# A graph attention layer on one core: TensorE fill-in work, run counts moved into the merges, shorter keys, and bins laid out by tile

## The chip, the cores and the metric

The kernel runs on one core of a Trainium2 chip. A core has five engines, each with its own instruction stream: TensorE (PE, matrix multiply; PEld is its weight load), VectorE (DVE), ScalarE (ACT), GpSimd (POOL) and SyncE (SP), which only issues transfers here. They share a fast memory of 128 partitions, TensorE writes into a separate accumulator memory (PSUM), and sixteen DMA engines move data to and from the chip's main memory (DRAM). The metric is the device time of one execution in microseconds (us); smaller is better.

## The reference

A graph attention layer with 4096 nodes, 50000 edges, 4 heads and 64 features in and out:

```python
x_proj[h] = x @ weight[h]
score[h, e] = sum(x_proj[h, src[e]] * att_src[h]) + sum(x_proj[h, dst[e]] * att_dst[h])
score = where(score > 0, score, 0.2 * score)
output[h, dst[e]] += exp(score[h, e]) * x_proj[h, src[e]]          # over all edges
output[h, dst]    /= sum(exp(score[h, e]) for e into dst) + 1e-8   # per node with edges
```

The result is the heads side by side, 4096 x 256, in float32.

## The kernel before

The kernel sorts the edges so that the work becomes matrix multiplies with one-hot matrices. The order of the work is the order in which the code issues it (a manual schedule); each engine runs its own stream in that order and waits on semaphores.

**Keys and first sort.** The edges' source and destination ids arrive in two halves, on SP's and ACT's queues. DVE makes one float key of each edge (L695 to L698, four instructions for each half): the high bits of the source (one of 16 source groups of 256 nodes), then the destination, then the low 8 bits of the source. Meanwhile ACT counts how many sources lie below each group's bound (`below`, L269). Then `Sorter.rows` sorts each partition's 391 keys with compare steps, and `Sorter.runs` merges eight partitions into one sorted run. A `half` step (L201) is two instructions, a minimum and a maximum over 128x256 elements, and the next step needs both. The loop over m (L245) has two stages, m = 1 and m = 2; each ends with nine `half` steps, or fewer when the last bits need no order (`fine`). A list `between` holds small closures; one is called after each of the last steps of stage m = 2.

**Where each group starts.** `counts` multiplies the counted signs with a selection matrix on TensorE (L280). `bounds` turns the result into start and end positions `ws1` and `we1`, by 14 small DVE instructions (L289 to L295). The sorted keys are stored to DRAM (L261, SP), `fetch` casts the positions to integers (L352), and GpSimd gathers each group's stretch of each run by two indirect transfers (L354).

**Tables.** Beside the first sort, `tables` makes on TensorE and ACT the node tables `xa` and `adb` that the matrix multiplies read later (L404 to L425).

**Second sort.** `group` merges the fetched stretches in the same way, so that each source group (16 of them, one to each tile) has its edges by destination. Here the small count steps already stand between the last merge steps, as do `relative` and `split`, which make the bins of block 0. TensorE runs 80 small matmuls into a tile `turn` (L372) before the counts of this sort and 5 wide ones into a tile `warm` (L377) behind them; their results are not used. `warm` and the counts share one PSUM buffer.

**Blocks.** The destinations are cut into 33 blocks of 125. An edge's bin is a pair (row: destination within the block; column: source within the group), and a block has 16 tiles of 128 edges each. For a block b:

- `load` (L472, SP) brings the block's bins to all partitions, 8 KB to each: 2 halves (row, column) x 16 tiles x 128. Blocks 0 and 1 get theirs through TensorE instead: `spread` (L483), with copies from PSUM by ACT or DVE (L485).
- `onehot` (DVE) compares the bins with the partition number: half 0 is one instruction over rows and columns (L498, 4096 elements), half 1 compares the columns again with the number plus 128 (L501, 2048 elements).
- `gather` (TensorE, L519, L521, L525, in three chunks of 6, 6 and 4 tiles) picks source features and scores; ACT takes `ex` (L527) and `xs` (L529) out of PSUM.
- `weights` (L539) and `values` (L547) on DVE make weighted features; `sums` (L563, L570) adds them up by destination into the PSUM tile `acc`; `take` (ACT, L624, L626), `project` (TensorE, L631), `invert` and `give` (DVE, L636, L644) finish a block, and SP stores it.

**The handover to the blocks.** The bins of blocks 2 and up pass through DRAM. GpSimd gathers five windows of the second sort's result (`Windows`, L354), window i for blocks 8i to 8i+7. `unpack(i)` splits a window into rows and columns (L442, L443 on DVE, L446, L447 on DVE for window 0 and on GpSimd for the others) and SP writes both to `gat_bins` (L449, two transfers to a window). The code from L729 on orders it: block 0 by `spread`, the windows, `longest` (L334 to L338), `unpack(0)`, loads of blocks 2 to 4, block 1 by `spread`, then `unpack(1)` to `unpack(4)`, `sums(0, 1)`, `onehot(2)`, and the loop `run(1)` over the other blocks. DVE's stream therefore has the four unpacks ahead of `onehot(2)`, and TensorE's first work for block 2 waits for that. The name `gather(b, c)` below means chunk c of block b.

Of the kernel before, what the change touches and what calls it, by code (L numbers as in the profile page):

```python
# [11 lines left out]
P = 128  # L12
# [9 lines left out]
L = 512  # L22
# [16 lines left out]
def kernel(ctx: ExitStack, tc: tile.TileContext, x: bass.AP, edge_index: bass.AP,  # L39
# [21 lines left out]
    skey2 = nc.dram_tensor("gat_sorted2", (1, P * L + W2), I32).ap()  # L61
    bin_dram = nc.dram_tensor("gat_bins", (8 * NI, 2, NR, W2), BF16).ap()

# [98 lines left out]
    adb = cst.tile([P, ND, AB], BF16)  # L162
    Wbd = cst.tile([P, 2, P], F32)
    ws1 = cst.tile([P, 2], F32)
    we1 = cst.tile([P, 2], F32)
# [6 lines left out]
    class Sorter:  # L172
# [58 lines left out]

        def runs(self, to=None, fine=0, between=()):

            s, d = self.step()
            V.stream_shuffle(out=self.z[:], in_=s[:], mask=[p ^ 1 for p in range(32)])
            V.tensor_scalar(out=self.y[:], in0=s[:], scalar1=sig[:, 0:1], scalar2=None, op0=OP.mult)
            V.scalar_tensor_tensor(out=d[:], in0=av(self.z[:], L - 1, [-1, L]), scalar=sig[:, 0:1], in1=self.y[:],
                                   op0=OP.mult, op1=OP.min)  # L240
            s, d = self.step()
            V.tensor_scalar(out=d[:], in0=s[:], scalar1=sj[0][:, 0:1], scalar2=None, op0=OP.mult)
            for j in range(8, -1, -1):
                self.half(j)
            for m in range(1, 3):  # L245
                self.turn()
                self.opposed(m)
                for j in range(m - 1, -1, -1):
                    self.half(j)
                self.turn()  # L250
                last = fine if m == 2 else 0
                todo = list(between) if m == 2 else []
                for j in range(8, last - 1, -1):
                    self.half(j, to=to if m == 2 and j == last else None)
                    if todo:
                        todo.pop(0)(self.a[self.cur])
                assert not todo
            return to or self.a[self.cur]
# [24 lines left out]

    def bounds(pool, cps, nt, n, off, mask, nk, ws, we):

        ni = ws.shape[1] // len(cps)
        for i, ps in enumerate(cps):
            cnt = pool.tile([P, nt + 1], F32, name=f"cnt{i}")
            V.tensor_scalar(out=cnt[:], in0=ps[:], scalar1=-0.5, scalar2=RUN * n / 2, op0=OP.mult, op1=OP.add)  # L289
            for o, t in ((0, ws), (1, we)):  # L290
                pick = pool.tile([P, ni, nk], F32, name=f"pick{i}{o}")
                V.tensor_tensor(out=pick[:], in0=av(cnt[:], o, [nk, ni], [1, nk]),
                                in1=av(mask[:], 0, [0, ni], [1, nk]), op=OP.mult)
                V.tensor_reduce(out=t[:, i * ni:(i + 1) * ni], in_=pick[:], axis=AX, op=OP.add)
                V.tensor_tensor(out=t[:, i * ni:(i + 1) * ni], in0=t[:, i * ni:(i + 1) * ni],  # L295
                                in1=av(off[:], i, [0, ni]), op=OP.add)

# [58 lines left out]

    PAGE = 80

    def group(pool, pp, start, between=()):

# [6 lines left out]
        so.rows(9)  # L367
        if between:

            turn = pp.tile([P, L], F32, name="turn")  # L370
            for i in range(PAGE):
                T.matmul(out=turn[:, 0:32], lhsT=identb[:], rhs=identb[:, 0:32], start=True, stop=True)  # L372
        st = Stretches(pool, counts(pool, pp, sgn, 8 * NI, [sel2[:]])[0])
        if between:
            warm = pp.tile([P, L], F32, name="warm")
            for i in range(5):
                T.matmul(out=warm[:], lhsT=identb[:], rhs=adb[:, 0:4, 0:P], start=True, stop=True)  # L377
        ki = pool.tile([P, L], I32, name="ki")
# [52 lines left out]
    class Windows:  # L431
# [7 lines left out]

        def unpack(self, i, *engs):  # L440
            t, tb = self.t[:, i], self.tb[:, i]
# [5 lines left out]
            e.tensor_scalar(out=tb[:, 0, :], in0=t[:, 0, :], scalar1=boff[:, i:i + 1], scalar2=None, op0=OP.add)  # L447
            for k, eng in enumerate(engs):
                eng.dma_start(out=dataclasses.replace(bin_dram[8 * i, k], ap=[[2 * NR * W2, 8], [W2, NR], [1, W2]]),  # L449
                              in_=self.tb[:, i, k, :])  # L450

# [5 lines left out]
    class Blocks:  # L457
# [11 lines left out]
        def load(self, b):  # L469
            if b < ND:  # L470
                t = self.bcp.tile([P, 2, NT * W2], BF16, name="bc")
                nc.sync.dma_start(out=t[:], in_=dataclasses.replace(bin_dram[b], ap=[[0, P], [NT * W2, 2],  # L472
                                                                                    [1, NT * W2]]))
                self.bc[b] = t

        def spread(self, b, c, tb, row, copy):

            if c == 0:
                self.bc[b] = self.bcp.tile([P, 2, NT * W2], BF16, name="bc")
            t0, n = CH[c]  # L480
            ps = self.psx.tile([P, CH[0][1], PW], F32, name="ps")
            for i in range(n):
                T.matmul(out=ps[:, i, :], lhsT=av(identb[:], row(t0 + i), [0, P]), rhs=tb, start=(i % 2 == 0),  # L483
                         stop=True, skip_group_check=True)
            copy(out=av(self.bc[b][:], t0 * W2, [W2, n], [NT * W2, 2], [1, W2]),  # L485
                 in_=av(ps[:], 0, [PW, n], [W2, 2], [1, W2]))

        def onehot(self, b, t0=0, nt=NT, halves=(0, 1)):
            if b >= ND:
                return  # L490
            if t0 == 0 and halves[0] == 0:

                self.oh[b] = self.bp.tile([P, 3, NT * W2], BF16, name="oh")
            oh, bc = self.oh[b], self.bc[b]
            e = slice(t0 * W2, (t0 + nt) * W2)
            for i in halves:
                if i == 0:
                    V.tensor_scalar(out=oh[:, 0:2, e], in0=bc[:, :, e], scalar1=pF[:, 0:1], scalar2=None,  # L498
                                    op0=OP.is_equal)
                else:  # L500
                    V.tensor_scalar(out=oh[:, 2, e], in0=bc[:, 1, e], scalar1=pF[:, 1:2], scalar2=None,  # L501
                                    op0=OP.is_equal)

        def gather(self, b, c):
# [9 lines left out]
            t0, n = CH[c]  # L514
            ps = self.psx.tile([P, CH[0][1], PW], F32, name="ps")
            for i in range(n):
                t = t0 + i
                e = slice(t * W2, (t + 1) * W2)
                T.matmul(out=ps[:, i, P:P + XC], lhsT=oh[:, 1, e], rhs=xa[:, 2 * t, :], start=(i % 2 == 0), stop=False,  # L519
                         skip_group_check=True)  # L520
                T.matmul(out=ps[:, i, 0:S0], lhsT=oh[:, 0, e], rhs=adb[:, b, :], start=False, stop=False,  # L521
                         skip_group_check=True)
            for i in range(n):
                t = t0 + i
                T.matmul(out=ps[:, i, P:P + XC], lhsT=oh[:, 2, t * W2:(t + 1) * W2], rhs=xa[:, 2 * t + 1, :],  # L525
                         start=False, stop=True, skip_group_check=True)
            S.activation(out=av(ex[:], 2 * t0, [2, n], [2 * NT, 2 * H], [1, 2]),  # L527
# [152 lines left out]
    with tc.tile_pool(name="sort1", bufs=1) as so1, tc.tile_pool(name="pre", bufs=1) as pr, \  # L680
            tc.tile_pool(name="pps", bufs=2, space=PSUM) as pps, \
            tc.tile_pool(name="pp1", bufs=1, space=PSUM) as pp1:
        sli = so1.tile([P, EL], I32)
        tF = so1.tile([P, EL], F32)
        uF = so1.tile([P, EL], F32)
# [5 lines left out]
        for e, n in ((0, EH), (EH, EL - EH)):  # L691
            src = av(eS[:], 2 * e, [2, n])
            dst = av(eD[:], 2 * e, [2, n])
            c = slice(e, e + n)
            V.tensor_scalar(out=sli[:, c], in0=src, scalar1=SG - 1, scalar2=None, op0=OP.bitwise_and)  # L695
            V.tensor_scalar(out=tF[:, c], in0=sli[:, c], scalar1=1.0 - N, scalar2=None, op0=OP.mult)
            V.scalar_tensor_tensor(out=uF[:, c], in0=dst, scalar=float(SG), in1=tF[:, c], op0=OP.mult, op1=OP.add)
            V.scalar_tensor_tensor(out=key[:, c], in0=src, scalar=float(N), in1=uF[:, c], op0=OP.mult, op1=OP.add)  # L698
        tables(pr, pps, pp1)
        so.rows(1, EL)  # L700
        cps = counts(so1, pp1, sgn, NR, [sel1[:, 0, :], sel1[:, 1, :]])
        store(skey1, so.runs())
        bounds(so1, cps, NR, EL, off1, m16, NR, ws1, we1)
    with ExitStack() as st:
# [3 lines left out]
        class Lent:  # L708


            def tile(self, shape, dt, name):
                return blocks.sink.psf.tile(shape, dt, name=name, tag="pf")


# [13 lines left out]

        stretches = group(so2, Lent(), ws1[:], (relative, split))  # L729
        win = Windows(cst, stretches.to[0][:])  # L730
# [6 lines left out]
        V.scalar_tensor_tensor(out=over[:], in0=most[:, 1:2], scalar=float(W2), in1=over[:], op0=OP.is_gt, op1=OP.max)  # L737
        win.unpack(0, nc.sync, nc.sync)
        for b in range(2, 5):
# [14 lines left out]
        for i in range(1, NI):  # L754
            win.unpack(i, nc.sync, nc.sync)
        blocks.sums(0, 1)
        blocks.onehot(2)
        blocks.weights(1)
# [5 lines left out]
    with tc.If(again > 0):  # L764
        n1 = room(0, EL)
        with tc.tile_pool(name="all", bufs=1) as al:
            total = al.tile([P, ND, AW], F32)
            V.memset(total[:], 0.0)
            with tc.For_i(0, n1, W1):
# [5 lines left out]
                with tc.For_i(0, m2, W2):  # L775
                    with ExitStack() as st:
                        win = Windows(st.enter_context(tc.tile_pool(name="win", bufs=1)), advance(al, ws2, we2, W2, 2)[:])
                        for i in range(NI):
                            win.unpack(i, nc.sync, nc.scalar)
                        blocks = Blocks(st, Total(total))  # L780
# [42 lines left out]
```

## Time and profile before

| | us |
|---|---|
| median of 4 runs | 292.77 |
| lowest and highest run | 291.27 and 293.16 |
| the profiled execution | 292.4 |
| its span (first to last instruction) | 290.4 |
| DVE busy in it | 261.4 (90%) |
| PE busy | 203.0 (70%) |
| ACT busy | 190.9 (66%) |
| POOL busy | 33.7 (12%) |

Times in the profile's views count from the start of the span; what lies around the span in the profiled execution is 2.0 us. A row of a timeline gives start, busy time, engine, source line, operation, tiles, and in brackets the idle time of the engine just before and what ended it. The chain of waits (part 4 of the page) has no entries in this profile, so the path has to be read from the rows of the engines.

### The profile page before, as it was taken

Reading aid. Unit: us, or ns where it says so; the run is one execution under the profiler, and the core shown is the slowest. Engines: PE = TensorE matmul, PEld = TensorE weight load, DVE = VectorE, ACT = ScalarE, POOL = GpSimd, SP = SyncE. Lnnn points to the kernel's source line nnn. Section 1 sums busy time; section 2 is a strip of 40 time slices with the busy share of each in tenths; the row PEclk is TensorE's granted clock in tenths of the full one; section 3 lists DMA queues with packets and bytes.
Section 4 is the critical chain, followed back from the end, with each engine's and each line's share of the span. In section 5 each row is a group of like instructions: output and inputs, shape, how many; then the busy total and the mean of one; then the engine's idle time right before and its main releaser. Section 6 shows DMA issues by size and latency. Waiting matters only on the chain.

```text
span 290.4 us, 8664 instructions
## 1 busy us (share of the span) xinstructions
PE 203.0 (70%) x3593; PEld 195.2 (67%) x3593; DVE 261.4 (90%) x528; ACT 190.9 (66%) x392; POOL 33.7 (12%) x81
## 2 busy tenths in 40 slices
PE   0001899990000017559999999999999999999980
PEld 0000599990000004459999999999999999999980
DVE  5999999996499999968999999999999999999960
ACT  2960720031499955755888888888888888888850
POOL 7882000000200000851000000000000000000000
PEclk9999975555555557997999999999999999999997
DMA  3026000001100000197776676768675767665011
GB/s 110 0 50 115 0 2 0 0 3 37 36 0 0 0 0 37 45 308 272 272 269 236 255 259 234 273 225 286 214 297 205 302 224 270 251 244 182 23 39 40
DMA packets 13328, 40.77 MB, mean 140 GB/s; under 512 B 3120, under 2 KB 8912, under 8 KB 9312
## 3 DMA queue, kind: packets, MB, share of 16 engines
q1 hardware_dynamic: 10768, 37.91, 36.0%
q10 hardware_dynamic: 1808, 1.56, 2.3%
q0 software_dynamic: 704, 0.66, 1.4%
q8 instruction: 30, 0.49, 0.7%
q14 instruction: 18, 0.15, 0.2%
HBM read 35.08 MB, written 5.05 MB: 138 GB/s over the span
## 4 chain that ended last, share of the span: by engine, by line


## 5 line engine op out<-in xcount | busy, mean ns | idle before, releaser
L529 ACT CAST xs<-ps 128x1200 bf16<-128x1200 f32 (+1 forms) x99 | 104.1, 1052 | 0.0
L547 DVE TENSOR_TENSOR val<-xs,wv 128x4096 bf16<-128x4096 bf16 (+1 forms) x34 | 75.4, 2221 | 0.4 <-ACT xs L529 0.2
L519 PE MATMUL ps<-xa,oh 128*128 128x72 bf16 x528 | 59.4, 197 | 5.0 <-DVE oh L498 3.4
L521 PE MATMUL ps<-adb,oh 128*128 128x136 bf16 x528 | 62.2, 225 | 0.0
L570 PE MATMUL acc<-xs,val 128*128 128x125 bf16 x1024 | 61.9, 218 | 0.0
L570 PEld LDWEIGHTS <-val 128*128 128x128 bf16 x1056 | 59.0, 98 | 0.1
L521 PEld LDWEIGHTS <-oh 128*128 128x128 bf16 x528 | 49.5, 99 | 1.7 <-issue 1.6
L519 PEld LDWEIGHTS <-oh 128*128 128x128 bf16 x528 | 47.3, 99 | 3.9 <-DVE oh L498 3.9
L498 DVE TENSOR_SCALAR oh<-bc,pF 128x4096 bf16<-128x4096 bf16 (+2 forms) x37 | 42.5, 1150 | 0.7 <-ACT bc L485 0.7
L527 ACT ACTIVATE ex<-ps 128x96 bf16<-128x96 f32 (+1 forms) x99 | 25.0, 252 | 24.8 <-PE ps L525 24.7
L201 DVE TENSOR_TENSOR sA<-sB 128x256 f32<-128x256 f32 (+2 forms) x104 | 37.2, 400 | 1.7
L201 DVE TENSOR_TENSOR sB<-sA 128x256 f32<-128x256 f32 (+2 forms) x98 | 35.1, 400 | 1.6
L525 PE MATMUL ps<-xa,oh 128*128 128x72 bf16 x528 | 33.7, 199 | 0.1
L280 PE MATMUL cnt_ps<-sgn,sel 128*128 128x17 f32 (+1 forms) x6 | 1.7, 390 | 40.1 <-ACT sgn L272 40.1
L280 PEld LDWEIGHTS cnt_ps<-sgn,sel 128*128 128x128 f32 x6 | 1.4, 319 | 40.1 <-issue 40.1
L525 PEld LDWEIGHTS <-oh 128*128 128x128 bf16 x528 | 26.6, 99 | 0.2 <-DVE oh L501 0.2
L501 DVE TENSOR_SCALAR oh<-bc,pF 128x2048 bf16<-128x2048 bf16 (+2 forms) x37 | 25.7, 694 | 0.0
L421 PEld LDWEIGHTS at_ps<-uv,xT 64*128 64x128 f32 x130 | 25.2, 302 | 0.2 <-issue 0.2
L421 PE MATMUL at_ps<-uv,xT 64*128 64x4 f32 x130 | 25.3, 331 | 0.0
L269 ACT ACTIVATE junk<-kr,nb 128x512 f32<-128x512 f32 x33 | 23.8, 722 | 1.1
L631 PE MATMUL pf<-Wbd,aT 128*128 128x128 f32 x132 | 22.8, 296 | 0.8 <-ACT aT L624 0.8
L404 PE MATMUL ps<-ident,wS 64*128 64x64 f32 x2 | 0.7, 350 | 27.9 <-DMA wS<-in_weight_dram 27.9
(144 smaller groups left out, 247.1 us busy)
## 6 DMA issues: line engine op xcount, KB each, us to landing
bc<-gat_bins SPq DMA_DIRECT2D x31, 1024.0 KB
out_dram<-res SPq DMA_DIRECT2D x32, 125.0 KB
eS<-in_edge_index_dram SPq DMA_DIRECT2D x2, 195.0 KB
eD<-in_edge_index_dram ACTq DMA_DIRECT2D x2, 195.0 KB
gat_bins<-tb SPq DMA_DIRECT2D x10, 32.0 KB
gat_sorted<-sA SPq DMA_DIRECT2D x1, 256.0 KB
gat_sorted<-ki SPq DMA_DIRECT2D x1, 256.0 KB
win<-gat_sorted,to POOLq DMA_INDIRECT x5, 2.6
```

The lines of the kernel that those rows point to most:

```text
L201: V.tensor_tensor(out=av(d[:], o, [2 * h, n], [1, h]), in0=av(s[:], 0, [2 * h, n], [1, h]), in1=av(s[:], h, [2 * h, n], [1, h]), op=op)
L269: S.activation(out=junk[:], in_=v, func=ACTF.Sign, bias=nbnd[:, b:b + 1], scale=1.0, accum_out=sgn[:, b:b + 1])
L421: T.matmul(out=ps[:, b, :], lhsT=xT[:, b * step:b * step + P], rhs=uv[:, k, :], start=(b == 0), stop=True, skip_group_check=True)
L498: V.tensor_scalar(out=oh[:, 0:2, e], in0=bc[:, :, e], scalar1=pF[:, 0:1], scalar2=None, op0=OP.is_equal)
L501: V.tensor_scalar(out=oh[:, 2, e], in0=bc[:, 1, e], scalar1=pF[:, 1:2], scalar2=None, op0=OP.is_equal)
L519: T.matmul(out=ps[:, i, P:P + XC], lhsT=oh[:, 1, e], rhs=xa[:, 2 * t, :], start=(i % 2 == 0), stop=False, skip_group_check=True)
L521: T.matmul(out=ps[:, i, 0:S0], lhsT=oh[:, 0, e], rhs=adb[:, b, :], start=False, stop=False, skip_group_check=True)
L525: T.matmul(out=ps[:, i, P:P + XC], lhsT=oh[:, 2, t * W2:(t + 1) * W2], rhs=xa[:, 2 * t + 1, :], start=False, stop=True, skip_group_check=True)
L527: S.activation(out=av(ex[:], 2 * t0, [2, n], [2 * NT, 2 * H], [1, 2]), in_=av(ps[:], P, [PW, n], [1, 2 * H], [0, 2]), func=ACTF.Exp)
L529: S.copy(out=xs[:, t0:t0 + n, 0:P + XC], in_=ps[:, 0:n, 0:P + XC])
L547: V.tensor_tensor(out=av(val[:], h * Dout, [Dout, n], [C, NT], [1, Din]), in0=av(xs[:], S0, [0, n], [XW, NT], [1, Din]), in1=av(wv[:], h * ...
L570: T.matmul(out=self.to[k], lhsT=val[:, t, k * P:(k + 1) * P], rhs=xs[:, t, 0:BD], start=apart and t == 0, stop=(t == NT - 1), skip_group_c ...
```

## The change

It has five parts.

1. **Keys.** The source's high bits are masked out in place of its low bits, so the key needs three instructions for each half, and the tile `tF` is gone.
2. **Counts.** `counts` of the first sort is issued to TensorE ahead of `tables`. `bounds` returns a list of 15 closures (the cast to integers `wi1` is the last) in place of running them; nine of them stand between the nine steps of stage m = 1 (`ahead`) and six between those of m = 2.
3. **TensorE.** The 80 small `turn` matmuls go. A function `busy(n)` issues n matmuls of 512 columns into a tile that shares its buffer with `acc`: 9 behind the counts of the second sort (5 before), 11 ahead of `unpack(0)`, where TensorE's stream goes on to `spread(1, ...)`, and 3 between `sums(0, 1)` and `gather(2, 0)`.
4. **Bins.** `gat_bins` and the tiles `bc` and `oh` are laid out by tile: 128 rows, then 128 columns, tile after tile. `unpack` writes a window by one transfer, 512 bytes to each partition, and `load` reads 8 KB in one piece where it read two of 4 KB. The copies behind `spread` become contiguous.
5. **One-hot.** Half 0 runs over one contiguous stretch. Half 1 reads the columns of `bc` in runs of 128 with gaps of 128 between them, and writes contiguously.

The diff, cut to its core:

```diff
-    bin_dram = nc.dram_tensor("gat_bins", (8 * NI, 2, NR, W2), BF16).ap()
+    bin_dram = nc.dram_tensor("gat_bins", (8 * NI, NR, 2, W2), BF16).ap()
...
-        def runs(self, to=None, fine=0, between=()):
+        def runs(self, to=None, fine=0, between=(), ahead=()):
...
-                todo = list(between) if m == 2 else []
+                todo = list(between if m == 2 else ahead)
...
-    def bounds(pool, cps, nt, n, off, mask, nk, ws, we):
+    def bounds(pool, cps, nt, n, off, mask, nk, ws, we, wi):
+        steps = []
...
-            V.tensor_scalar(out=cnt[:], in0=ps[:], scalar1=-0.5, scalar2=RUN * n / 2, op0=OP.mult, op1=OP.add)
+            steps.append(lambda cnt=cnt, ps=ps: V.tensor_scalar(
+                out=cnt[:], in0=ps[:], scalar1=-0.5, scalar2=RUN * n / 2, op0=OP.mult, op1=OP.add))
...
+        steps.append(lambda: V.tensor_copy(out=wi[:], in_=ws[:]))
+        return [lambda keys, f=f: f() for f in steps]
...
-            turn = pp.tile([P, L], F32, name="turn")
-            for i in range(PAGE):
-                T.matmul(out=turn[:, 0:32], lhsT=identb[:], rhs=identb[:, 0:32], start=True, stop=True)
         st = Stretches(pool, counts(pool, pp, sgn, 8 * NI, [sel2[:]])[0])
         if between:
-            warm = pp.tile([P, L], F32, name="warm")
-            for i in range(5):
-                T.matmul(out=warm[:], lhsT=identb[:], rhs=adb[:, 0:4, 0:P], start=True, stop=True)
+            busy(9)
...
-            for k, eng in enumerate(engs):
-                eng.dma_start(out=dataclasses.replace(bin_dram[8 * i, k], ap=[[2 * NR * W2, 8], [W2, NR], [1, W2]]),
-                              in_=self.tb[:, i, k, :])
+            nc.sync.dma_start(out=bin_dram[8 * i:8 * i + 8].rearrange("b g k e -> (b g) k e"), in_=tb)
...
-                t = self.bcp.tile([P, 2, NT * W2], BF16, name="bc")
-                nc.sync.dma_start(out=t[:], in_=dataclasses.replace(bin_dram[b], ap=[[0, P], [NT * W2, 2],
-                                                                                    [1, NT * W2]]))
+                t = self.bcp.tile([P, 2 * NT * W2], BF16, name="bc")
+                nc.sync.dma_start(out=t[:], in_=dataclasses.replace(bin_dram[b], ap=[[0, P], [1, 2 * NT * W2]]))
...
-            copy(out=av(self.bc[b][:], t0 * W2, [W2, n], [NT * W2, 2], [1, W2]),
-                 in_=av(ps[:], 0, [PW, n], [W2, 2], [1, W2]))
+            copy(out=self.bc[b][:, t0 * PW:(t0 + n) * PW], in_=av(ps[:], 0, [1, n * PW]))
...
-                    V.tensor_scalar(out=oh[:, 0:2, e], in0=bc[:, :, e], scalar1=pF[:, 0:1], scalar2=None,
-                                    op0=OP.is_equal)
+                    e = slice(2 * t0 * W2, 2 * (t0 + nt) * W2)
+                    V.tensor_scalar(out=oh[:, e], in0=bc[:, e], scalar1=pF[:, 0:1], scalar2=None, op0=OP.is_equal)
                 else:
-                    V.tensor_scalar(out=oh[:, 2, e], in0=bc[:, 1, e], scalar1=pF[:, 1:2], scalar2=None,
-                                    op0=OP.is_equal)
+                    V.tensor_scalar(out=av(oh[:], (2 * NT + t0) * W2, [W2, nt], [1, W2]),
+                                    in0=av(bc[:], (2 * t0 + 1) * W2, [2 * W2, nt], [1, W2]),
+                                    scalar1=pF[:, 1:2], scalar2=None, op0=OP.is_equal)
...
-            V.tensor_scalar(out=sli[:, c], in0=src, scalar1=SG - 1, scalar2=None, op0=OP.bitwise_and)
-            V.tensor_scalar(out=tF[:, c], in0=sli[:, c], scalar1=1.0 - N, scalar2=None, op0=OP.mult)
-            V.scalar_tensor_tensor(out=uF[:, c], in0=dst, scalar=float(SG), in1=tF[:, c], op0=OP.mult, op1=OP.add)
-            V.scalar_tensor_tensor(out=key[:, c], in0=src, scalar=float(N), in1=uF[:, c], op0=OP.mult, op1=OP.add)
+            V.tensor_scalar(out=sli[:, c], in0=src, scalar1=2 * N - SG, scalar2=None, op0=OP.bitwise_and)
+            V.scalar_tensor_tensor(out=uF[:, c], in0=sli[:, c], scalar=float(N - 1), in1=src, op0=OP.mult, op1=OP.add)
+            V.scalar_tensor_tensor(out=key[:, c], in0=dst, scalar=float(SG), in1=uF[:, c], op0=OP.mult, op1=OP.add)
+        cps = counts(so1, pp1, sgn, NR, [sel1[:, 0, :], sel1[:, 1, :]])
         tables(pr, pps, pp1)
         so.rows(1, EL)
-        cps = counts(so1, pp1, sgn, NR, [sel1[:, 0, :], sel1[:, 1, :]])
-        store(skey1, so.runs())
-        bounds(so1, cps, NR, EL, off1, m16, NR, ws1, we1)
+        steps = bounds(so1, cps, NR, EL, off1, m16, NR, ws1, we1, wi1)
+        store(skey1, so.runs(ahead=steps[:9], between=steps[9:]))
...
+        def busy(n):
+            t = blocks.psa.tile([P, L], F32, name="warm", tag="acc")
+            for i in range(n):
+                T.matmul(out=t[:], lhsT=identb[:], rhs=adb[:, 0:4, 0:P], start=True, stop=True)
...
+        busy(11)
+        win.unpack(0)
...
             win.unpack(i)
         blocks.sums(0, 1)
+        busy(3)
         blocks.onehot(2)
```

## The prediction

> **What bounds the kernel now.** I read the busy tenths first, then DVE's groups by shape, then the timeline around the two sorts and the handover.
>
> ```profile
> span 290.4 us, 8664 instructions
> ...
> PE   0001899990000017559999999999999999999980
> ...
> DVE  5999999996499999968999999999999999999960
> ...
> PEclk9999975555555557997999999999999999999997
> ```
>
> A slice is 7.26 us. DVE is full except at the start, around 70 us (slices 10 and 11), around 120 to 135 (17 to 19) and at the end. The granted clock is half from slice 6 to slice 15 and dips again in slice 18. In the loop from about 142 us DVE has no idle time; a block takes 4.71 us and PE, full too, 4.70. So I follow DVE to 142 us; what it gains until then, the end gains, unless an instruction in the loop becomes dearer.
>
> **The keys.** The second half of the ids starts its first key step at 5.42, behind its transfer. Four instructions become three. One costs 0.3 in a queue (4.01 to 4.31 in the timeline), and two halves make 0.6. But the second half can't start much before its data: 0.30 if it starts where it did, 0.60 if it follows at once. I take -0.45. ACT's counting waits only for the ids.
>
> **The counts of the first sort.** The timeline between the sorts:
>
> ```profile
> 67.99 0.17 DVE L289 TENSOR_SCALAR cnt<-cnt_ps 128x17 f32<-128x17 f32 x1
> 68.10 0.34 SPq L261 DMA_DIRECT2D gat_sorted<-sA  x1
> ...
> 71.28 0.17 DVE L352 CAST wi<-ws 128x2 int32<-128x2 f32 x1 [0.43 <-issue]
> 72.29 1.06 POOL L354 DMA_INDIRECT raw<-gat_sorted,wi  x1 [48.39 <-DVE wi L352]
> ```
>
> The merge ends at 68.07 and the gather starts 4.22 later, behind 15 small DVE instructions. With these gone the gather waits for the store alone. The second sort's store shows that wait: issued 113.45, its gather at 116.18, 2.73 later. The 15 now lie between merge steps. A merge pair costs 0.80 without an instruction between its steps (105.16 to 105.95) and 0.79 to 0.81 with one, in the second sort: the step waits for its predecessor anyhow. I allow 0 to 0.15 for all. The counts' matmuls, moved ahead of the tables on PE, wait for ACT's counting, which ends at 19.1; PE's first table work waits for a transfer until 27.94, so nothing is queued behind them that could start. ACT's table copies end at 66.7, ahead of the gather's new time of about 70.6. Gain 4.22 - 2.73 - 0.1, rounded to -1.3 (bounds -1.0 and -1.5). The second sort starts 1.75 earlier.
>
> **TensorE before block 0.** The `turn` matmuls run at 63.43 to 65.72 behind the first counts, off every path. Five `warm` wait for DVE's count (2.03 idle) and run 108.42 to 110.71:
>
> ```profile
> 108.40:111.80 3.40, 3.38 (x11) 1.50 (x11) 3.40 (x14) 0.41 (x1) 0.00 (x0) 0.50 0.00 0
> 111.80:115.20 3.40, 1.78 (x18) 1.27 (x17) 2.75 (x9) 3.08 (x3) 0.00 (x0) 0.98 0.21 80
> ...
> 128.80:132.20 3.40, 1.03 (x19) 0.89 (x20) 2.70 (x6) 0.13 (x1) 2.78 (x3) 1.00 1.00 414
> 132.20:135.60 3.40, 3.40 (x53) 3.34 (x52) 3.40 (x3) 2.02 (x4) 0.00 (x0) 0.53 0.57 174
> ```
>
> (Busy time of PE, weight loads, DVE, ACT, POOL; then granted clock, DMA share, GB/s.) The clock follows the stretch before: PE full at 0.50, then 0.98; PE at 1.03 of 3.40, then 0.53. It changes at 40.09, 111.77, 132.25 and 135.66, whole multiples of 3.41 apart. Nine matmuls without the wait for `cnt` start at about 104.5 and run 9 x 0.427 = 3.84, to 108.3; the bins of block 0 come at 108.9. If the clock is up by then, `spread(0)` (2.06 at half clock), whose copies DVE waits for, is shorter. DVE's idle there is 0.26 and 0.39 ahead of one-hots, and window 0's landing caps the gain: 0 to -0.45. I take -0.25. The Trainium skill ("TensorE: Matmul & The Clock Gate", Part 1) lets the clock rise after a free-running window of 3413 ns of work; 3.84 us covers such a window whole only in (3.84 - 3.41)/3.41, 13%, of positions. By that rule this term is nothing and the sum 0.25 worse.
>
> **busy(11) in front of spread(1).** These stand ahead of `spread(1)` in PE's queue, and ACT's copies, DVE's `onehot(1)` and PE's own `gather(1)` follow it. At full clock, where the clock is 1.00 in that stretch, a matmul costs half of 0.43: 11 x 0.216 = 2.37. They start when `longest` leaves PE and end at about 118.8, against bins of block 1 ready at 117.9. ACT's copy follows 0.89 later (120.06 to 120.95), the one-hot 1.47 after that (122.42): 121.1, where DVE could be at 120.4. That is +0.7 (bounds 0 and +0.8). Here DVE stands at -1.3 against before.
>
> **The stall before unpack(4).**
>
> ```profile
> 121.26 2.00 POOL L354 DMA_INDIRECT win<-gat_sorted,to  x1 [0.30 <-issue]
> ...
> 122.74 2.10 SPq L472 DMA_DIRECT2D bc<-gat_bins  x3
> ...
> 129.40 0.23 DVE L442 TENSOR_SCALAR t<-win 128x128 int32<-128x128 int32 x1 [2.51 <-DMA win<-gat_sorted,to]
> ```
>
> Window 4 is issued at 121.26 and its data takes 8.1 us to land; the other windows take 2.5 to 2.6. Its gather took 2.00 where the others took 0.94 to 0.99, and three loads of 1 MB each were issued before it had landed. DVE waits 2.51 us with `onehot(2)` queued behind, and PE 3.43 us at `gather(2, 0)`. After the change all gathers start 1.75 earlier, while the one-hots and loads come 1.3 and some 2.5 earlier: one bins transfer stands before the loads instead of two (1.37 for the two on SP's queue, so about 0.65 less). DVE arrives at 126.8 - 1.3 = 125.5. Clear of the loads the window lands at 121.26 - 1.75 + 2.6 = 122.1: no stall. If it stays at its distance of 6.6 behind the loads, issued at 120.05 to 120.5, it lands at 126.7 to 127.1: a stall of 1.2 to 1.6. I take 0.8, the middle, since both rows are of this place: -1.7. `onehot(2)` starts at 129.68 - 3.0 = 126.7.
>
> **busy(3).** It needs the buffer that `take(0)` leaves, at 128.93 - 1.3 = 127.65, and takes 0.65: 128.3, where half 0 of `onehot(2)` ends at 128.05. PE loses 0.25. From `gather` to `weights` a block takes 4.13 at full clock (274.20 to 278.33), so `weights(2)` is ready at 132.4; DVE comes at 136.35 - 0.72 - 3.0 = 132.6. Cost 0, at most 1.1 if the stall is gone altogether (the two then cancel in part).
>
> **The clock after it.**
>
> ```profile
> 136.35 0.23 DVE L539 TENSOR_TENSOR wv<-ex 128x128 bf16<-128x128 bf16 x1 [0.72 <-ACT ex L527]
> ...
> 141.55 0.23 DVE L539 TENSOR_TENSOR wv<-ex 128x128 bf16<-128x128 bf16 x1 [0.52 <-ACT ex L527]
> ```
>
> These two waits come from the half-clock stretch at 132.2. PE's gap shrinks from 3.43 to about 1.3 and then busy(3), so the clock should stay up: -0.72 - 0.52 = -1.24 (0 if it drops anyway).
>
> **Bins and one-hots.** The loads carry the same bytes, hidden behind four blocks' work. Half 0 becomes contiguous. Half 1 now hops between runs of 128:
>
> ```profile
> L547 DVE TENSOR_TENSOR val<-xs,wv 128x4096 bf16<-128x4096 bf16 x32 | 73.1, 2283 | 0.2
> L498 DVE TENSOR_SCALAR oh<-bc,pF 128x4096 bf16<-128x4096 bf16 x31 | 39.1, 1262 | 0.0
> L501 DVE TENSOR_SCALAR oh<-bc,pF 128x2048 bf16<-128x2048 bf16 x31 | 23.3, 751 | 0.0
> L498 DVE TENSOR_SCALAR oh<-bc,pF 128x1536 bf16<-128x1536 bf16 x4 | 2.5, 616 | 0.7 <-ACT bc L485 0.7
> ```
>
> (Count, busy us and mean ns.) The same operation at 1536 elements is already two runs of 768 a half tile apart, on both sides, and (1262 - 616)/2560 gives 0.252 ns an element, the rate that half 1 has between 768 and 2048. So hops cost nothing there, and I take 0. The bound above is `val`, which reads rows of 64: 0.518 ns from its forms of 2048 and 4096, or +0.545 an instruction. The skill's "VectorE: DVE Perf Modes" (Rules for kernel authors) asks for dense step-1 data for the top rate; its tiers (estimate from 693 and 1224 ns at 2048 elements) would add 31 x 0.53 = 16.5 us. The measured 1536 form speaks against that reading.
>
> **Sum.** -0.45 - 1.3 - 0.25 + 0.7 - 1.7 + 0 - 1.24 + 0 = -4.24. The profiled execution took 292.4 (span 290.4 and 2.0 around it), so 288.2; the median of the runs is 0.4 above it, which the range covers.
>
> **Rivals.**
>
> A, busy(11) at half clock. If the nine don't lift the clock and `spread(0)` and `longest` don't hold it, 11 x 0.43 = 4.7 us, 2.4 more on DVE's path; the earlier windows hide nothing of it but remove the stall. Net about -1.9: 290.5. Against it: before, the clock was up from 111.8 with less work. 9%.
>
> B, the stall stays. The loads come closer to the gathers than before, as SP has one transfer less ahead of them. With the old 2.51 kept the sum is -2.5, 289.9; with window 4 behind all three loads DVE may wait 5 us more than I count, near 293. The first is likelier. 6%.
>
> C, the other side: half 1 loses its rate. At `val`'s slope it costs 31 x 0.545 = +16.9, all on DVE, which is full: 292.4 - 4.2 + 16.9 = 305.1. It decides from 4.24/31 = 0.137 us an instruction, that is 0.751 becoming 0.888. For it: runs of 128 are six times shorter than the 768 measured. 7%.
>
> D, the early gains don't arrive: DVE's path to 142 us is set by something I have not seen, such as window or load transfers that start no earlier. Each gain up to 121 us then ends in the stall, and with the clock dip kept the time stays near 292. 8%.
>
> **How the numbers follow.** Forecast 70%, with its own range 286.8 to 289.8: the stall wholly gone (-0.8), or counts, keys and `spread(0)` at their better ends (-0.55), against the full 1.6 of stall and half the clock's 1.24. A and the first of B reach to 291.0; C, D and the worse of B lie above. Below 286.8 several better ends must meet. A difference of 0.5%, 1.46 us, is about what a measurement of this kernel can tell. Faster than 291.3: 0.69 of the forecast, 0.07 of A, 0.04 of B, 0.80. Same: most of D, 0.08. Slower: C, the rest, 0.12.
>
> **What the next profile would show.** Right: `raw` gathered near 70.5 with no DVE work between merge and store; half-1 one-hots at 0.75; `spread(1)` near 118.8; idle before unpack(4) under 1.6; no half clock after 112; no wait at `weights(2)` and `weights(3)`. Wrong: half 1 above 0.85; busy(11) at 4.7 us; a window that lands later than 127; a loop period above 4.71.

## The result, and the profile after

The changed kernel takes 291.63 us (median of 44 runs, 289.38 to 293.58), the kernel before 292.35 (70 runs): a ratio of 0.9978, 95% interval 0.9964 to 0.9992. A second comparison, told below as a run of its own, gave 0.9939 (0.9907 to 0.9970). So the change gains 0.7 to 1.8 us, where 4.2 were forecast, and the median lies above the stated range. Some executions of these kernels ran in a slower state, 2 to 6 us longer; the medians below are of the others.

The profiled execution took 289.42 us and is one of the fastest of the changed kernel: it is 3.0 below the profiled execution of before, but 2.2 below its own median. What its trace shows is one draw, and the experiments' traces are needed beside it. From the page:

```profile
span 287.5 us, 8530 instructions
...
PE   0010899980000045879999999999999999999990
...
DVE  5999999994499999779999999999999999999970
...
PEclk9999975555555559899999999999999999999998
```

Slices are counted from 0. The two idle slices of DVE around 70 us (9 and 10) are still there. By the clock records in the trace the clock comes up at 107.52, where it came up at 111.92 before; it is at half once more from 114.35 to 117.76 (the 8 in slice 16), and the dip in slice 18 is gone. The timeline has the handover:

```profile
67.82 0.34 SPq L262 DMA_DIRECT2D gat_sorted<-sA  x1
70.85 1.06 POOL L362 DMA_INDIRECT raw<-gat_sorted,wi  x1 [47.24 <-issue]
...
120.05 1.90 POOL L362 DMA_INDIRECT win<-gat_sorted,to  x1 [0.30 <-issue]
...
120.25 1.27 SPq L469 DMA_DIRECT2D bc<-gat_bins  x3
...
122.09 0.62 DVE L493 TENSOR_SCALAR oh<-bc,pF 128x1536 bf16<-128x1536 bf16 x1 [0.96 <-ACT bc L481]
...
128.47 0.27 DVE L441 TENSOR_SCALAR t<-win 128x128 int32<-128x128 int32 x1 [1.97 <-DMA win<-gat_sorted,to]
...
134.47 0.22 DVE L534 TENSOR_TENSOR wv<-ex 128x128 bf16<-128x128 bf16 x1
```

The bracket is the idle time ahead and what ended it. The loads were issued 2.5 us earlier than before, but window 4 landed only 0.9 earlier (128.45 against 129.37, its last event), and DVE still waits for it. The milestones, from the same rows of both profiles:

| | before | after | moved |
|---|---|---|---|
| gather of the first sort's stretches | 72.29 | 70.85 | -1.44 |
| second sort starts (its data landed) | 76.61 | 75.53 | -1.08 |
| its result is stored | 113.45 | 112.31 | -1.14 |
| unpack(0) | 119.24 | 117.88 | -1.36 |
| loads of blocks 2 to 4 issued | 122.74 | 120.25 | -2.49 |
| unpack(1) | 126.00 | 125.60 | -0.40 |
| unpack(4) | 129.40 | 128.47 | -0.93 |
| weights(3) | 141.55 | 139.22 | -2.33 |
| span's end | 290.4 | 287.5 | -2.9 |

### The profile page after: what moved, and what is told of

Read it like the earlier page. It is cut to its first block, busy times and chain, and to the rows that moved or that the text cites. A ratio compares the mean times of both kernels' runs of the same rounds, so it can differ in the third digit from the quotient of the medians.

```text
span 287.5 us, 8530 instructions
## 1 busy us (share of the span) xinstructions
PE 204.8 (71%) x3531; PEld 194.9 (68%) x3531; DVE 259.1 (90%) x526; ACT 191.0 (66%) x392; POOL 33.3 (12%) x81
## 4 chain that ended last, share of the span: by engine, by line
## 5 line engine op out<-in xcount | busy, mean ns | idle before, releaser
L420 PEld LDWEIGHTS at_ps<-uv,xT 64*128 64x128 f32 x130 | 26.0, 311 | 0.2 <-issue 0.2
L420 PE MATMUL at_ps<-uv,xT 64*128 64x4 f32 x130 | 26.1, 337 | 0.0
L558 PEld LDWEIGHTS <-xs 128*128 128x128 bf16 x528 | 18.6, 96 | 0.4
```

The costliest lines, as they stand in the source:

```text
L420: T.matmul(out=ps[:, b, :], lhsT=xT[:, b * step:b * step + P], rhs=uv[:, k, :], start=(b == 0), stop=True, skip_group_check=True)
```

## The experiments

Three theories stood first. Theory 1: the early gain is real, and TensorE's fill-in work gives it back. Theory 2: the new layout of the bins gives it back, by holding up a window. Theory 3: the early gain is swallowed by the wait for window 4. The first four runs take the parts one by one and repeat the whole; they shared the runs of the kernel before (292.7).

**e1_front: keys and counts alone** (parts 1 and 2; the rest as before).

```diff
-        stretches = group(so2, Lent(), ws1[:], (relative, split))
+        stretches = group(so2, Lent(), wi1[:], (relative, split))
...
-        store(skey1, so.runs())
-        bounds(so1, cps, NR, EL, off1, m16, NR, ws1, we1)
+        steps = bounds(so1, cps, NR, EL, off1, m16, NR, ws1, we1, wi1)
+        store(skey1, so.runs(ahead=steps[:9], between=steps[9:]))
```

> The kernel before with the keys and the counts of the change alone. Theory 1 (the early gain is real and TensorE's fill-in work gives it back): raw gathered about 1.4 us earlier, the second sort's store 1.1 earlier, and the time 1.0 to 1.3 below the kernel before (ratio about 0.996). Theory 2 (the bins layout gives it back): the same. Theory 3 (the early gain is swallowed by the wait for window 4, which hangs on transfers that do not move): within 0.3 of the kernel before, with the wait ahead of unpack(4) longer by about 1.

Measured: 291.07, a ratio of 0.9921 (0.9882 to 0.9961), 1.6 by the medians. Its profiled execution took 292.78, the longest of those counted. The store of the second sort is at 112.32, as in the changed kernel. Theory 3 is out: the early gain arrives.

**e2_pe: the TensorE part alone** (part 3).

```diff
-            turn = pp.tile([P, L], F32, name="turn")
...
-            for i in range(5):
-                T.matmul(out=warm[:], lhsT=identb[:], rhs=adb[:, 0:4, 0:P], start=True, stop=True)
+            busy(9)
...
+        busy(11)
         win.unpack(0, nc.sync, nc.sync)
...
+        busy(3)
```

> The kernel before with the TensorE part alone (no turn, 9, 11 and 3 wide matmuls). Theory 1: busy(11) delays onehot(1) by 0.7 to 1.0 in every execution, while the clock is only sometimes up earlier: time 0 to 1 us above the kernel before. Theory 2: the delay is paid back by the removed clock dip (1.2): 0.3 to 0.6 below. Theory 3: within 0.3, as the delay is swallowed by the wait ahead of unpack(4).

Measured: 293.97, 1.3 above by the medians; the ratio, 1.0022 (0.9990 to 1.0054), does not settle the sign. No gain of its own: theory 1 as far as it goes.

**e3_bins: the layout alone** (parts 4 and 5).

```diff
-    bin_dram = nc.dram_tensor("gat_bins", (8 * NI, 2, NR, W2), BF16).ap()
+    bin_dram = nc.dram_tensor("gat_bins", (8 * NI, NR, 2, W2), BF16).ap()
...
-        win.unpack(0, nc.sync, nc.sync)
+        win.unpack(0)
```

> The kernel before with the bins and one-hots by tile alone. Theory 1: nothing in the loop (half 1 stays at 0.75 us), the wait ahead of unpack(4) within 0.5 of 2.5: time within 0.4 of the kernel before. Theory 2: the loads, issued sooner behind one bins transfer, hold up window 4 by 0.5 to 1.5 more: time 0.5 to 1.5 above. Theory 3: within 0.4.

Measured: 292.5, a ratio of 0.9991 (0.9962 to 1.0019): nothing, so theory 2 fails as a matter of this part alone. In its trace, and in that of e1_front, no window was waited for; both show DVE waiting for TensorE instead. In e1_front's timeline:

```profile
116.95 0.54 PE L345 MATMUL mx_ps<-ident,mxr 128*1 128x128 f32 x2
...
119.58 0.41 DVE L346 TENSOR_REDUCE most<-mx_ps 1x2 int32<-1x256 f32 x1 [2.42 <-remote]
```

TensorE's record of the maxima ends at 117.5, DVE gets them 2.1 later. That put off unpack(0) and with it the loads, to 123.9, and the windows landed in the clear by 123.0. The late load of block 2 then cost a wait of 1.71 at `onehot(2)`.

**e4_again: the changed kernel once more,** without an edit.

> The changed kernel once more, for a second execution in the trace. Theory 1: a slower execution than the profiled 289.4, about 291.6, whose trace shows the clock up later than 107.3 or another dip between 107 and 136, and the difference lies between 109 and 142 us. Theory 2: the same clock, but window 4 landing later than 128.4. Theory 3: a loss elsewhere, before 105 us.

Measured: 291.43 (12 runs), and a profiled execution of 291.7, 2.3 above the first one. Its timeline:

```profile
127.65 0.23 DVE L441 TENSOR_SCALAR t<-win 128x128 int32<-128x128 int32 x1 [1.66 <-DMA win<-gat_sorted,to]
...
129.30 0.23 DVE L441 TENSOR_SCALAR t<-win 128x128 int32<-128x128 int32 x1 [1.28 <-DMA win<-gat_sorted,to]
...
136.54 0.23 DVE L534 TENSOR_TENSOR wv<-ex 128x128 bf16<-128x128 bf16 x1 [1.02 <-ACT ex L522]
```

Two windows are late here, 3 and 4: a stall of 2.94 in all, more than before's 2.51. And a half-clock stretch is back from 131.21, behind which `weights(2)` waits the 1.02. The wait at `onehot(1)` is 0.84, close to the first execution's 0.96. So the slower execution has both, theory 1's dip and theory 2's late window.

So the question became what makes the windows late. Theory A: their packets queue behind the 3 MB of loads that the change itself issues earlier. Theory B: the loads are not the cause. C and D are about the fill-in work: that busy(11) costs its whole delay, and that the fill-in work holds the clock up. The next four ran together (before: 292.5).

**e5_load2: one load ahead of the windows.**

```diff
-        for b in range(2, 5):
-            blocks.load(b)
+        blocks.load(2)
...
             win.unpack(i)
+            if i == 1:
+                blocks.load(3)
+                blocks.load(4)
```

> The changed kernel with only the load of block 2 ahead of the windows' landing; the loads of blocks 3 and 4 are issued behind unpack(1). Theory A (window 4 is late because its packets queue behind 3 MB of loads that the change issues earlier): window 4 lands about 124, no wait ahead of unpack(4), onehot(2) at 126.4 in place of 128.8; busy(3) then sets gather(2,0) at about 129.4, so the time is 0.7 to 1.5 below the changed kernel, about 290.3. Theory B (window 4 is late through its own gather or the clock, not the loads): the wait stays at 1.5 to 3 us and the time within 0.4.

Measured: 292.32, a ratio of 0.9989 (0.9967 to 1.0012): a miss on the time, a hit on the window. The windows were unpacked without a wait (by the trace's events window 4's data had landed at 124.9). But the load of block 3 now stood behind unpack(1)'s transfer on SP's queue, went out at 130.85, and became the new wait:

```profile
136.03 1.28 DVE L493 TENSOR_SCALAR oh<-bc,pF 128x4096 bf16<-128x4096 bf16 x1 [2.44 <-DMA bc<-gat_bins]
```

DVE came late itself, after a wait of 2.63 at `onehot(1)`, so that the windows were in time proves little; that window 4 landed at 124.9, not at 128.5, fits A. Holding the loads back only moves the wait.

**e6_late4: unpack(4) behind onehot(2).**

```diff
-        for i in range(1, NI):
+        for i in range(1, NI - 1):
             win.unpack(i)
...
         blocks.weights(1)
+        win.unpack(NI - 1)
```

> The changed kernel with unpack(4) moved behind onehot(2) and weights(1). Theory A: windows 3 or 4 still land at 128 to 129, but onehot(2) no longer stands behind the last of them; where only window 4 is late, onehot(2) starts at 126.2 unless its own load (1 MB in 4 us) holds it; gather(2,0) again waits for busy(3) at 129.4: 0.5 to 1.3 below the changed kernel. Theory B: the wait goes to the load of block 2 or to unpack(3): within 0.4.

Measured: 291.02, a ratio of 0.9940 (0.9916 to 0.9964): 0.4 to 0.6 below the changed kernel by the medians, but with the same ratio as e4_again (0.9939), so no gain is shown. In its trace TensorE's results were late again (a wait of 1.60 for the maxima, 1.26 for the copy), so `onehot(2)` started at 128.40 and the windows were in time. The run does not tell A from B.

**e7_nobusy11: without the 11.**

```diff
-        busy(11)
```

> The changed kernel without the 11 wide matmuls ahead of unpack(0). Theory A: the wait of onehot(1) for ACT's copy (0.96 and 0.84 in two executions) goes, but DVE only arrives earlier at unpack(4), whose window hangs on the loads: onehot(2) moves by less than 0.4, and the time by -0.5 to +0.3. Theory C (the 11 cost their full 0.9 to the end): 0.7 to 1.0 below the changed kernel. Theory D (they hold the clock up): spread(1) at half clock and the time 0.5 to 1.5 above.

Measured: 289.88, but a ratio of 0.9941 (0.9912 to 0.9970), the same as e4_again's 0.9939: inconclusive as to time. Its trace is A's: the wait at `onehot(1)` is gone, unpack(1) is at 124.66, and DVE then waits 2.04 and 1.35 for windows 3 and 4; `onehot(2)` starts at 129.32, 0.5 later than in the profiled execution of after. What comes in earlier waits longer.

**e8_load2_nb3: as e5_load2, without busy(3).**

```diff
-        busy(3)
```

> As the run with one load ahead, and without the three wide matmuls between sums(0,1) and gather(2,0). Theory A: gather(2,0) starts with onehot(2)'s half 0 at about 127.7, weights(2) at 132.3 in place of 134.5: 2 us below the changed kernel, about 289.5, if the clock stays up without busy(3) as TensorE's gap is short. Theory D (busy(3) holds the clock): a half-clock stretch after 130 and no gain over the run with busy(3).

Measured: 292.34, a ratio of 1.0011 (0.9993 to 1.0028). The late load of block 3 is in it as well (2.17), so busy(3) can't be judged from it.

Of the last four (before: 292.6), three leave the loads where they are and take both late windows off DVE's path; e11_nobusy3 asks after busy(3) alone.

**e9_late34: unpack(3) and unpack(4) behind the values of block 1, no busy(3).**

```diff
-        for i in range(1, NI):
+        for i in (1, 2):
             win.unpack(i)
         blocks.sums(0, 1)
-        busy(3)
...
-        blocks.run(1)
+        blocks.run(1, lambda: [win.unpack(i) for i in range(3, NI)])
```

(`run` calls it once, behind its first `values`.)

> The changed kernel with unpack(3) and unpack(4) moved behind the values of block 1 and without busy(3); busy(11) stays. Theory A (the wait for the late windows, and behind it busy(3), are what holds gather(2,0)): onehot(2) at 126 and gather(2,0) at 127.3 where TensorE is not late itself; weights(2) about 132.3 in place of 134.5: 1.5 to 2.2 below the changed kernel, about 289.5. Theory B (the load of block 2 or TensorE's own late results hold onehot(2) or gather(2,0) at 128 or later): 0 to 0.8 below.

Measured: 287.98, a ratio of 0.9838 (0.9795 to 0.9881), 4.6 below the kernel before. The timeline:

```profile
125.57 1.32 DVE L493 TENSOR_SCALAR oh<-bc,pF 128x4096 bf16<-128x4096 bf16 x1
...
126.94 0.21 PE L514 MATMUL ps<-xa,oh 128*128 128x72 bf16 x1 [0.16 <-DVE oh L493]
...
132.05 0.21 DVE L534 TENSOR_TENSOR wv<-ex 128x128 bf16<-128x128 bf16 x1
```

Windows 3 and 4 landed as late as ever (127.4 and 128.7 by their last events), and nobody waits. `gather(2, 0)` follows without a gap, and the clock stays up from 107.65 to the end of the loop. Theory A's numbers hold: `weights(2)` was expected at 132.3 and came at 132.05; the time was even lower than the expected 289.5.

**e10_late34_no11: the same without busy(11).**

```diff
-        busy(11)
```

> As the run before it, and without busy(11). Theory A (busy(11) delays onehot(1) and with it all that follows, now that no window hides it): onehot(2) at 125.2, weights(2) about 131.5 to 132: another 0.5 to 0.9 lower, about 288.8. Theory D (without the 11 the clock falls for spread(1) and gather(1)): no gain or a loss of up to 0.5 against the run before it.

Measured: 287.98 again, a ratio of 0.9849 (0.9804 to 0.9895). Without the 11 the clock is at half from 118.77 to 122.18, and `spread(1)` takes 2.43 in place of 1.47; `onehot(1)` starts at 121.13 against 121.51. By these six runs each the 11 are worth nothing either way (D, without a loss): what they cost in time they seem to give back in clock.

**e11_nobusy3: the changed kernel without busy(3) alone.**

```diff
-        busy(3)
```

> The changed kernel without busy(3) alone. Theory A: gather(2,0) waits for onehot(2), which waits for the windows, so busy(3) hides behind them: within 0.4 of the changed kernel. Theory D (busy(3) keeps the clock up behind the wait): the half-clock stretch after 130 comes in most executions and the time is 0.5 to 1.2 above.

Measured: 292.35, a ratio of 0.9982 (0.9953 to 1.0011), 0.7 to 0.9 above the changed kernel by the medians; by the ratios (0.9978 and 0.9939 there) the two are not separated. The windows view over the stretch where TensorE waits for `onehot(2)` (columns as in the prediction) reads, for this kernel:

```profile
128.43:131.85 3.42, 0.46 (x10) 0.46 (x11) 2.18 (x4) 0.00 (x0) 1.89 (x2) 1.00 0.73 269
```

and the clock is at half behind it, from 131.85: `weights(2)` waits 1.07 at 136.97. This fits theory D for busy(3), but e4_again lost its clock at nearly the same place (131.21) with busy(3), so that busy(3) is of use is not shown.

**e12_front_late34: keys, counts and the late unpacks, no TensorE part, old bins.**

```diff
         win = Windows(cst, stretches.to[0][:])
...
-        for i in range(1, NI):
+        for i in (1, 2):
             win.unpack(i, nc.sync, nc.sync)
...
-        blocks.run(1)
+        blocks.run(1, lambda: [win.unpack(i, nc.sync, nc.sync) for i in range(3, NI)])
```

> The kernel before with keys, counts and the late unpack(3) and unpack(4): no TensorE part, no new bins layout. Theory A (what the change gains is its front, what it leaves is the windows): about 289.5, 1.5 to 2 below the run with the front alone. Theory D (the TensorE part is needed for the clock): 290.5 or more.

Measured: 290.73, a ratio of 0.9938 (0.9910 to 0.9966): 2.7 above e9_late34. Its timeline says where:

```profile
121.56 2.07 SPq L480 DMA_DIRECT2D bc<-gat_bins  x3
...
127.59 1.29 DVE L506 TENSOR_SCALAR oh<-bc,pF 128x4096 bf16<-128x4096 bf16 x1 [2.10 <-DMA bc<-gat_bins]
```

With two bins transfers ahead of them the loads go out at 121.56, not at 120.18 as in e9_late34, and `onehot(2)` waits 2.10 for its own. From the first bins transfer to the loads it is 2.76 here and 1.72 in e9_late34, so about 1.0 of the 1.4 is the second transfer. The single transfer thus helps where the windows are not waited for, by how much no run isolates; in the changed kernel it also brings the loads closer to the gathers (to window 4's, from 1.44 behind it here to 0.20). TensorE's share of the 2.7 was not taken apart.

**What decides whether a window is late** can be read from all 14 traces, which hold 70 window gathers. Time to land is counted here from a gather's issue to the end of its last packet; the last event comes about 0.35 later.

| gather issued, against the first load of the bins | gathers | time to land, us |
|---|---|---|
| more than 2.2 us ahead | 51 | 2.1 to 2.6 |
| 1.44 to 1.67 ahead | 12 | four 2.2 to 2.4, eight 5.0 to 8.4 |
| 0.2 to 0.3 ahead | 2 | 8.1; 4.7 in e5_load2, with one load in place of three |
| 1.6 to 1.8 behind | 5 | 6.3 to 7.2 |

The kernels differ in their TensorE work, their bins and their clock, and the distance to the loads sorts the windows all the same. So the loads make the windows late, as theory A has it; the gather or the clock alone, theory B, would not sort them so. In between the distance does not decide. Window 3 stood 1.45 ahead of the loads in the profiled execution of after and 1.48 ahead in e9_late34; it landed in 2.2 in the first and in 8.4 in the second:

```profile
118.80 0.94 POOL L362 DMA_INDIRECT win<-gat_sorted,to  x1 [0.30 <-issue]
```

```profile
118.70 2.99 POOL L362 DMA_INDIRECT win<-gat_sorted,to  x1 [0.30 <-issue]
```

Of the six traces whose three loads went out between 120.0 and 120.6 (after, e4, e7, e9, e10, e11) it was late in five; the profiled execution of after is the sixth. Whether the late packets stand in line behind those of the loads, or GpSimd is late in handing them over, the traces leave open.

## Why the prediction was wrong

**Keys and counts** were right in kind and near in size: -1.75 forecast, -1.6 by e1_front's median, -1.08 in the trace where the second sort starts. The keys gave 0.28 in place of 0.45, since the second half still starts at 5.43, when its data lands, which was the lower bound. The wait from store to gather was 3.03 in place of 2.73, and the gathered data took 4.68 to arrive, 0.36 longer than before.

**spread(0)** gave 0.22 (the move from the second store to unpack(0)), 0.25 forecast. **busy(11)** cost 0.96 and 0.84 in the two traces, 0.7 forecast; rival A, all 11 at half clock and 2.4 more, showed in neither, though the first two ran at half clock in the profiled execution (2.95 us for the 11, 2.54 in e4_again).

**The stall before unpack(4) is the step that failed.** I took the middle of "clear of the loads" and "as far behind them as before", 0.8, a gain of 1.7. Measured: 1.97 in one execution and 2.94 in the other, 0.5 less and 0.4 more than before. The window was to land at 122.1 to 127.1 and DVE to come at 125.5. In the profiled execution DVE came at 126.5, the early gains being smaller and busy(11) dearer, and the window landed at 128.45. The old distance of 6.6 us from loads to window was no bound: it was 8.2 (120.25 to 128.45) and 8.7 (120.56 to 129.27 in e4_again). The prediction had the mechanism as rival B with 6%, and had noticed that the loads gain 0.65 on the gathers; it should have read that as the likelier case. In the profile of before window 4, issued 1.48 ahead of the loads, was already late, and window 3, 2.73 ahead, was not; the change brings them to 0.20 and 1.45, where both can be late. B's first sum, 289.9, was still too low, because it left the next term whole.

**The clock's 1.24** hung on the same stall. It came in the profiled execution and not in e4_again, which waits longer. The windows view over the clock window before that place in each, after first, then e4_again:

```profile
128.00:131.41 3.41, 2.08 (x24) 1.35 (x24) 2.83 (x6) 0.77 (x5) 3.29 (x5) 1.00 0.88 336
```

```profile
127.79:131.21 3.42, 1.00 (x7) 0.39 (x7) 2.14 (x6) 0.57 (x3) 2.49 (x4) 1.00 0.87 326
```

TensorE busy for 2.08 of 3.41: the clock stayed. Busy for 1.00: it fell. (The prediction's times of the clock's changes, 40.09 to 135.66, are 0.15 early; the trace's clock records have 40.24, 111.92, 132.40 and 135.82, the same whole multiples of 3.41 apart.)

With -1.6, -0.22, +0.9, a stall that changes by -0.5 to +0.4, and -1.24 or nothing, the sum is -2.7 to -0.5, around the -0.7 to -1.3 measured by the medians. The forecast's last 2.9 us, stall and clock, exist: e9_late34 got them by taking the windows off the path; that its 287.98 lies near the 288.2 forecast for the changed kernel is in part luck, as it also lacks busy(3) and its early gains were smaller than forecast.

**Half 1** was right: 0.749 us in 31 instructions, 0.751 before.

```profile
L495 DVE TENSOR_SCALAR oh<-bc,pF 128x2048 bf16<-128x2048 bf16 x31 | 23.2, 749 | 0.0
```

Rival C falls by it, and with it the dense-data rule of the Trainium skill ("VectorE: DVE Perf Modes", Rules for kernel authors) as a reason against runs of 128 elements. **Rival D**, that the early gains are swallowed, was true in part, by B's mechanism.

What stays open: why TensorE's results reach the others one to three us late in six of the fourteen traces (e1, e2, e3, e5, e6, e8), at different places between 116 and 124 us. It happens with and without the TensorE part. It shifts the loads, and so bears on which windows are late; that it is a part of the 4 us over which the runs of one kernel spread is likely, but not shown.

## What to carry to other kernels

Before a stall is counted as gained, list every transfer that shares its DMA engines and ask which of them the change brings forward: a small gather that landed in 2.6 us when clear took about 8 when it was issued 0.2 us ahead of three large loads, and all 51 issued more than 2.2 us ahead were in time. Where a late transfer can't be made earlier, move its consumer behind work that doesn't need it: here that was worth 3.5 us, together with leaving out busy(3), five times the change itself by its first comparison. And one profiled execution is one draw: here it lay 2.2 us below its kernel's median, three times the difference that was found.

## What the runs showed of the hardware

The clock window need not be full. In the changed kernel the clock rose at 107.52 behind this window, in e4_again at 107.31 behind one with 2.94, and in e8_load2_nb3 at 113.56 behind one with 2.91:

```profile
104.11:107.52 3.41, 3.15 (x9) 1.48 (x10) 3.31 (x9) 0.16 (x1) 0.00 (x0) 0.50 0.00 0
```

The busy time of a window does not decide alone: 2.69 (e6_late4, e8_load2_nb3) and twice even 3.12 (e3_bins, e7_nobusy11) left the clock at half. So did seven full windows running in the changed kernel, on the tables' matmuls of 4 columns (L420), and at least five in every other trace:

```profile
39.25:63.14 23.89, 23.89 (x114) 23.89 (x113) 23.24 (x70) 0.44 (x2) 0.00 (x0) 0.50 0.00 1
```

From 95 us on it fell behind every window with less than 1.47, and between 1.47 and 1.80 it went either way. In eight of the ten traces with busy(9) the clock was up by 110.3, in the four without it at 110.7 to 113.8. The Trainium skill ("TensorE: Matmul & The Clock Gate", Part 1) asks for a sustained window to rise and an idle one to fall, from which the prediction worked out 13%; these traces agree with the window of 3.41 us and not with either condition.

A GpSimd gather issued just ahead of the loads can hold GpSimd longer, too. The ten window gathers that were issued 0.2 to 1.67 us ahead of the first load and landed late took 1.90 to 3.00 us there; all the others took 0.94 to 1.17, the five issued behind the loads, which landed late as well, among them.
